# A trunk of one layer on one core: the head by steps, gate stores two products later, part loads by GpSimd, normalising in steps

## The chip, the cores and the metric

The kernel runs on one core of a Trainium2 chip. The metric is the time of one execution on the device in microseconds (us). The five engines of a core are named as the profile names them: PE (matrix products), DVE (vectors), ACT (activations and casts), POOL (GpSimd) and SP (which here only issues transfers). Each engine runs its own instructions in the order of its queue; semaphores tie the queues together.

## The reference

One layer of a decoder trunk over 2048 positions of width 1024, in float32:

```python
mod = silu(c) @ w_ada + b_ada                       # 3 x 1024
shift, scale, gate = split(mod, 3)
u = x * (1 + scale) + shift
q, k, v, a_gate, p_in, p_gate, m_a, m_p = split(u @ w_in)
a = sliding_window_sink_attention(q, k, v, sinks, bias, mask) * silu(a_gate)
a = a @ w_attn_proj
p = einsum('bsgc,gcd->bsgd', multiscale_causal_pool(p_in), w_pool_mix)
p = ((p * pool_scale) * silu(p_gate)) @ w_pool_proj
y = (sigmoid(m_a) * a + sigmoid(m_p) * p) @ w_out * (1 + gate)
x = layer_norm(2 ** 0.25 * x + y, ln_gain, ln_bias)
```

The attention has 16 query heads of width 64, two key and value heads, a window of 128, a bias by distance and one sink per head. The pool is a causal mean over 2, 4, 8 or 16 positions less the position itself.

## The kernel before

**Products.** Every large matrix product is done by seven half-size products instead of eight, in the manner of Strassen and Winograd. The activation side is held as seven "sets" (B11, T1, T2, B21, T3, B22, T4: blocks of the input and differences of blocks), the weight side is combined per use. A `Quad` is the work of two weight tiles of 128 columns: it loads their four parts (A11, A21, A22, then A12 in `mid`, line 281), POOL combines them (lines 275, 279, 280, 285), ACT and DVE split each combination into a high and a low part in a reduced format (ACT's cast at line 307, DVE's subtract at line 128), and PE multiplies 12 times 128x512 per product. `front` does the products B11 and T1 of a quad, `back` the other five of each quad of a group. A group is two quads, 14 products. After each product `tick` runs the hooks that were planned for this place.

**Phases.** Each half of the sequence (1024 positions) goes through a gates phase (g0, g1: attention gate, pool gate and the two merge gates are computed, activated and stored to memory), and an attention phase (a0, a1: queries are computed, attention is done in blocks, the pool runs beside it on DVE and POOL). Then the mix phases project attention and pool results of both halves, and the output phase multiplies with `w_out` in four groups and normalises the rows. At each boundary the seven sets of the next phase are filled or built, half by half, at planned ticks.

**Order of the work.** A scheduler orders what is issued as `nc.sync`, `nc.scalar`, `nc.vector`, `nc.gpsimd`. What is issued through `sp`, `act`, `dve`, `pool` is kept in program order. Tiles come from pools with tags: the tag "c" has five buffers in turn, "p" four, "spare" two, "wide0" to "wide7" one each; a new tile waits until the old content of its buffer has been read or stored.

**Head.** `head` computes `silu(c)`, then for k = 0 to 7 the shift and the scale of 128 channels: the shift by 16 matmuls of one column on PE into one PSUM bank (`sums`), the scale as a row sum on DVE (`tensor_tensor_reduce`), each added to the bias in `mod`. ACT modulates x with them. From k and k+4 the parts of the sets follow: `sets_a` (B11, T1), `sets_b` (B21, T2), `sets_c` (B22, T3, T4), each split by ACT and DVE, the differences made by POOL. `products(i)` runs those matmuls of the first four products whose channels are there. `bias_rows` writes the attention's bias rows by 32 small POOL operations and stores them.

**Gates, A12, rows.** `gate_quad` activates a product's result on ACT (line 456), finishes it on DVE (lines 458, 460) and stores it on SP (line 461). `mid` issues the A12 load on SP behind POOL's subtract of line 279 or 280. In the output phase `out_quad` loads a row tile z when its first half is there (line 503), adds the product (line 508), and with the second half done goes through the whole normalisation at once: sum (ACT, 512), mean and its negative (DVE), squares (ACT, 516), power (POOL, 518), scaling with gain and bias (DVE, 519 and 520), store (ACT's queue, 521).

## Time and profile before

Three executions took 1890.62, 1895.62 and 1894.25 us, the median is 1894.25 us.

| what | value |
|---|---|
| profiled execution, its own time | 1898.95 us |
| its span | 1897.2 us |
| mean granted clock of PE | 0.968 |
| busy: PE, DVE, ACT, POOL | 92%, 69%, 50%, 49% |
| instructions | 25359 |
| bytes moved by DMA | 381.33 MB |

A row of a timeline has its start, its duration, the engine, the line, the operation, the tile it writes and those it reads, the shapes and how often it runs in sequence; in brackets stands how long the engine was idle before and what ended that. A row of the waits has the engine, the tile and line that waited, what it waited for, then the total in us, how many times, and the longest. A window has the busy time of PE, PEld, DVE, ACT and POOL in that stretch, with the number of instructions, then the granted clock, the share of the DMA engines and GB/s. In the kernel many operations are recorded under one helper line (55), so that tile names tell them apart: `pv`, `pt`, `lg`, `mm` are PSUM banks, `w_set` the split weights, `W` and `A` their raw parts, `set_B` and `set_T` the sets, `sig` the gates, `wide` the rows.

### The profile page before, as it was taken

The numbers are of one execution on the slowest core, as the hardware profiler recorded it, in microseconds if no ns is written. First come the engines' busy times: TensorE is split into PE (matmuls) and PEld (weight loads), VectorE is DVE, ScalarE is ACT, GpSimd is POOL, SyncE is SP. The second block draws the span as 40 slices with busy tenths as digits, with TensorE's granted clock in tenths as the row PEclk, the third lists the DMA queues.
The fourth block names the chain that finished last, engine by engine and source line by source line (L and its number), as shares of the span: only waits on it lengthen the run. The fifth ranks groups of instructions, "written<-read, shape, count | busy, mean of one in ns | idle before, by whom it ended". The sixth has DMA issues, their size and how long they took to land. (4 is left out here: it accounts for less than half of the span.)

```text
span 1897.2 us, 25359 instructions
## 1 busy us (share of the span) xinstructions
PE 1748.8 (92%) x8248; PEld 1446.6 (76%) x8248; DVE 1301.5 (69%) x2261; ACT 942.3 (50%) x1974; POOL 923.7 (49%) x724
## 2 busy tenths in 40 slices
PE   4589999999999999899999999999989989999996
PEld 4467777777888887677777888888867768777775
DVE  4767675564677776677665457777758987857776
ACT  3444434343777776444444457777725333423443
POOL 3544444441254666435354324457743764566542
PEclk9689999999999999999999999999989999999998
DMA  6344656568254447676767733543776574588332
GB/s 244 128 172 177 233 183 233 201 247 216 87 161 151 146 158 275 243 252 220 255 242 268 248 119 128 167 167 117 285 266 240 197 244 164 197 323 319 144 134 89
DMA packets 167284, 381.33 MB, mean 201 GB/s; under 512 B 19680, under 2 KB 23792, under 8 KB 167152
## 3 DMA queue, kind: packets, MB, share of 16 engines
q1 hardware_dynamic: 156288, 348.72, 52.7%
q0 software_dynamic: 5472, 17.85, 2.6%
q10 hardware_dynamic: 5392, 13.14, 2.0%
q8 instruction: 65, 1.06, 0.2%
q14 instruction: 67, 0.55, 0.1%
HBM read 244.35 MB, written 138.44 MB: 202 GB/s over the span
## 5 line engine op out<-in xcount | busy, mean ns | idle before, releaser
L55 PE MATMUL mm<-set_B,w_set 128*128 128x512 f32 x3240 | 813.3, 399 | 29.5 <-DVE w_set L128 25.1
L55 PEld LDWEIGHTS mm<-set_B,w_set 128*128 128x128 f32 x3240 | 610.0, 191 | 163.9 <-DVE w_set L128 34.2
L55 PE MATMUL lg<-set_T,w_set 128*128 128x512 f32 x2088 | 527.7, 402 | 59.2 <-DVE w_set L128 24.6
L55 PEld LDWEIGHTS lg<-set_T,w_set 128*128 128x128 f32 x2088 | 397.4, 193 | 166.7 <-DVE w_set L128 39.0
L128 DVE TENSOR_TENSOR w_set<-W,w_set 128x1024 fp32r<-128x1024 f32 x164 | 236.1, 1439 | 99.3 <-ACT w_set L307 89.7
L307 ACT CAST w_set<-W 128x1024 fp32r<-128x1024 f32 x164 | 171.8, 1048 | 218.2 <-PE mm L55 148.3
L55 PE MATMUL mm<-set_T,w_set 128*128 128x512 f32 x1080 | 268.8, 397 | 0.0
L55 PEld LDWEIGHTS mm<-set_T,w_set 128*128 128x128 f32 x1080 | 204.0, 191 | 42.6
L285 POOL TENSOR_TENSOR W<-W 128x512 f32<-128x512 f32 x58 | 79.9, 1377 | 169.1 <-DVE w_set L128 164.5
L279 POOL TENSOR_TENSOR W<-W 128x512 f32<-128x512 f32 x56 | 88.0, 1571 | 142.7 <-DVE w_set L128 122.9
L55 DVE TENSOR_TENSOR o<-pv,o 64x128 f32<-64x128 f32 x256 | 72.2, 282 | 99.6 <-ACT o L55 95.6
L358 POOL TENSOR_TENSOR p<-p,u 128x512 f32<-128x512 f32 x58 | 87.2, 1505 | 96.1 <-DVE u L357 91.8
L55 ACT ACTIVATE L<-L,nm 128x257 f32<-128x257 f32 (+1 forms) x256 | 127.1, 498 | 8.8 <-DVE nm L55 3.5
L55 DVE TENSOR_TENSOR k_lo<-spare,k_hi 128x512 fp32r<-128x512 f32 x88 | 83.9, 957 | 65.6 <-ACT k_hi L55 31.9
L275 POOL TENSOR_TENSOR W<-W,A 128x512 f32<-128x512 f32 x56 | 80.0, 1429 | 87.6 <-DMA W<-in_win_dram 23.8
L55 DVE CUSTOM_DVE_ANT_0 L<-lg,bt,nsink 128x256 f32<-128x256 f32 (+1 forms) x256 | 111.6, 473 | 5.3 <-PE lg L55 1.3
L55 POOL TENSOR_TENSOR w_set<-W,w_set 128x1024 fp32r<-128x1024 f32 x14 | 33.7, 2408 | 146.5 <-ACT w_set L55 108.5
L280 POOL TENSOR_TENSOR W<-W 128x512 f32<-128x512 f32 x56 | 90.9, 1623 | 22.9 <-DMA W<-in_win_dram 19.7
L55 POOL TENSOR_TENSOR p<-nxt,pg 128x512 f32<-128x512 f32 x32 | 41.3, 1292 | 123.2 <-DVE sm L55 113.6
L55 ACT COPY o<-pv 64x256 f32<-64x256 f32 x128 | 47.2, 369 | 80.6 <-PE pv L55 76.4
L55 DVE TENSOR_TENSOR ptl<-pt,pth 128x512 fp32r<-128x512 f32 (+1 forms) x128 | 85.6, 669 | 1.7 <-ACT pth L55 1.6
L55 ACT CAST k_hi<-spare 128x512 fp32r<-128x512 f32 x88 | 53.9, 616 | 60.3 <-POOL spare L55 29.7
(168 smaller groups left out, 2524.6 us busy)
## 6 DMA issues: line engine op xcount, KB each, us to landing
W<-in_win_dram SPq DMA_DIRECT2D x102, 256.0 KB, 3.8
w_set<-wmix_d SPq DMA_DIRECT2D x32, 512.0 KB, 5.4
A<-in_win_dram SPq DMA_DIRECT2D x34, 256.0 KB, 4.0
ag_d<-sig SPq DMA_DIRECT2D x32, 256.0 KB, 2.7
pg_d<-sig SPq DMA_DIRECT2D x32, 256.0 KB, 3.3
ma_d<-sig SPq DMA_DIRECT2D x32, 256.0 KB, 3.0
mp_d<-sig SPq DMA_DIRECT2D x32, 256.0 KB, 3.5
pg<-pg_d SPq DMA_DIRECT2D x32, 256.0 KB, 3.9
```

Of the source, the lines that this page charges most:

```text
L55: return lambda *args, **kw: self.tc.keep_in_program_order(op(*args, **kw))
L128: engine.tensor_tensor(dst, src, as32(hi), ALU.subtract)
L275: e.tensor_tensor(x[:, 1, :], x[:, 2, :], self.a22, ALU.add)
L279: e.tensor_tensor(x[:, 1, :], x[:, 1, :], x[:, 0, :], ALU.subtract)
L280: e.tensor_tensor(x[:, 2, :], x[:, 0, :], x[:, 2, :], ALU.subtract)
L285: nc.gpsimd.tensor_tensor(x[:, 0, :], x[:, 0, :], x[:, 1, :], ALU.subtract)
L307: a.copy(by_two(hi), raw)
L358: nc.gpsimd.tensor_tensor(p5, p5, u2, ALU.add)
```

## The change

- **Head.** `sets_a`, `sets_b`, `sets_c` are replaced by one loop over i = 0 to 3, in which the steps of one pair (i, i+4) stand between those of the next: `minus`, `parts`, `rest_sums`, `rest_parts`. PE's sums go to four banks in turn (`pv`, `pt`, `lg`, `lg`), and for k = 3 and 7 DVE does them instead. The loads of x land in tiles of other tags. `bias_rows` moves to the fourth tick of the first group of gates, in program order on POOL, its load to SP.
- **Gates.** The store of a gate is deferred by two ticks (`defer`, `run_due`) and issued in program order on SP.
- **A12.** `mid` issues the load through GpSimd.
- **Normalising.** `norm_row` does one step per tick: sum, squares, power, scale, store, in program order on each engine, the store on SP. Six rows are loaded at the start of the phase (`load_z`), each next one three ticks after a store, into six tiles in place of five. The scratch of the squares is a "spare" tile.
- **Order of tiles.** At the start of the mix T3 is allocated ahead of T4, and wide4 to wide7 at once; in attention the second pool part comes one step later, but for the last.

```diff
-        def mid(self, q=nc.sync, e=nc.gpsimd):
+        def mid(self, q=nc.gpsimd, e=nc.gpsimd):
...
+    now, due = [0], []
+    def defer(ticks, f):
+        due.append((now[0] + ticks, len(due), f))
+    def run_due(every=False):
+        while due and (every or any(d[0] <= now[0] for d in due)):
+            d = min(due, key=lambda d: d[:2])
+            due.remove(d)
+            d[2]()
...
+            now[0] += 1
+            run_due()
...
-        return after(tick) if after else None
+        result = after(tick) if after else None
+        if not (after and nxt):
+            run_due(True)
+        return result
...
-            nc.sync.dma_start(gates_d[name][s, m + mi, t], g)
+            defer(2, lambda: sp.dma_start(gates_d[name][s, m + mi, t], g))
...
+    zs = {}
+    def load_z(ph, row):
+        if row < S // P:
+            zs[row] = [wide(ph, 2 + row % 6), 0]
+            sp.dma_start(zs[row][0], xr[row * P : (row + 1) * P, :])
+    def norm_row(ph, row, z):
+        def small(name):
+            return ph.t.tile([P, 1], F32, tag=name, bufs=2, name=name)
+        total, mean, down, rs = (small(x) for x in ("total", "mean", "down", "rs"))
+        def sums():
+            act.activation(z, z, AF.Copy, accum_out=total)
+        def squares():
+            dve.tensor_scalar(mean, total, 1.0 / D, None, ALU.mult)
+            dve.tensor_scalar(down, total, -1.0 / D, None, ALU.mult)
+            act.activation(ph.spare(), z, AF.Square, bias=down, accum_out=rs)
+        def power():
+            dve.tensor_scalar(rs, rs, 1.0 / D, EPS, ALU.mult, ALU.add)
+            pool.tensor_tensor(rs, rs, mhalf, ALU.pow)
+            dve.scalar_tensor_tensor(z, z, mean, vec["gain"], ALU.subtract, ALU.mult)
+        def scale():
+            dve.scalar_tensor_tensor(z, z, rs, vec["lnb"], ALU.mult, ALU.add)
+        def store():
+            sp.dma_start(out[row * P : (row + 1) * P, :], z)
+            defer(3, lambda: load_z(ph, row + 6))
+        for at, f in ((1, sums), (2, squares), (3, power), (4, scale), (5, store)):
+            defer(at, f)
     def out_quad(k):
-        zs = {}
-        def small(ph, name):
-            return ph.t.tile([P, 1], F32, tag=name, bufs=2, name=name)
         def consume(ph, mi, n, src):
-            r0 = (k + mi) * P
-            if mi not in zs:
-                z = wide(ph, 2 + (k + mi) % 5)
-                nc.sync.dma_start(z, xr[r0 : r0 + P, :])
-                zs[mi] = [z, 0]
-            z = zs[mi][0]
-            zs[mi][1] += 1
+            z, n_done = zs[k + mi]
+            zs[k + mi][1] += 1
             zn = z[:, n * CH : (n + 1) * CH]
             nc.vector.scalar_tensor_tensor(zn, zn, ALPHA, src, ALU.mult, ALU.add)
-            if zs[mi][1] < 2:
-                return
-            total, mean, down, rs = (small(ph, x) for x in ("total", "mean", "down", "rs"))
-            nc.scalar.activation(z, z, AF.Copy, accum_out=total)
-            nc.vector.tensor_scalar(mean, total, 1.0 / D, None, ALU.mult)
-            nc.vector.tensor_scalar(down, total, -1.0 / D, None, ALU.mult)
-            sq = wide(ph, 7)
-            nc.scalar.activation(sq, z, AF.Square, bias=down, accum_out=rs)
-            nc.vector.tensor_scalar(rs, rs, 1.0 / D, EPS, ALU.mult, ALU.add)
-            nc.gpsimd.tensor_tensor(rs, rs, mhalf, ALU.pow)
-            nc.vector.scalar_tensor_tensor(z, z, mean, vec["gain"], ALU.subtract, ALU.mult)
-            nc.vector.scalar_tensor_tensor(z, z, rs, vec["lnb"], ALU.mult, ALU.add)
-            nc.scalar.dma_start(out[r0 : r0 + P, :], z)
+            if n_done:
+                norm_row(ph, k + mi, z)
...
-        act.dma_start(rel, relT)
+        nc.sync.dma_start(rel, relT)
         et = ph.t.tile([HEADS, ET], F32, tag="c", bufs=ph.bufs["c"], name="et")
-        nc.gpsimd.memset(et, BIG)
+        pool.memset(et, BIG)
...
-            nc.gpsimd.tensor_scalar(
+            pool.tensor_scalar(
                 et[:, lo_t : hi_t + 1], rel[:, b : b + 1].to_broadcast([HEADS, n]), -1.0, None, ALU.mult
             )
-        nc.gpsimd.dma_start(e_d, et)
+        pool.dma_start(e_d, et)
...
-                if n % U == 4 + 2 * st and (j, st) in sums:
+                if n % U == ((4, 6 + (j + 1 < KT))[st]) and (j, st) in sums:
...
-        cg = ph.p("cg"), ph.p("cg")
+        cg = [t for t in (places[5][:, 0:CH], places[5][:, CH:])]
...
-        bias_rows(ph)
-        sums = bank("pv")
         ws, xs, ts = {}, {}, {}
+        by_pe = (0, 4, 1, 5, 2, 6)
...
-            sp.dma_start(ws[k][0], wadat[k])
+            sp.dma_start(ws[k][0], (wadat if k in by_pe else wada)[k])
...
-            if k < 4:
-                xs[k] = (ph.spare(),)
-                sp.dma_start(xs[k][0], xt[0, k])
-            else:
-                xs[k] = ph.p("b21"), ph.p("b22")
-                for h, x in enumerate(xs[k]):
-                    sp.dma_start(x, cols(xt[0, k], h))
+            if k in (0, 1, 6):
+                t = ph.spare()
+                xs[k] = cols(t, 0), cols(t, 1)
+                sp.dma_start(t, xt[0, k])
+                return
+            xs[k] = [ph.p("x") if k in (4, 5, 7) else ph.c("x") for h in range(2)]
+            for h, x in enumerate(xs[k]):
+                sp.dma_start(x, cols(xt[0, k], h))
+        sums = {}
+        def pe_modulation(k):
+            if k not in by_pe:
+                return
+            sums[k] = bank(("pv", "pt", "lg", "lg")[by_pe.index(k) % 4])
+            for i in range(KT):
+                mm(sums[k][:, 0:1], ws[k][0][:, i * P : (i + 1) * P], ct[:, i : i + 1], start=i == 0, stop=i == KT - 1)
         def modulation(k):
-            wt, wa = ws.pop(k)
-            for i in range(KT):
-                mm(
-                    sums[:, k : k + 1],
-                    wt[:, i * P : (i + 1) * P],
-                    ct[:, i : i + 1],
-                    start=i == 0,
-                    stop=i == KT - 1,
-                    skip_group_check=True,
-                )
+            for m, wa in ((KT + k, ws[k][1]), (k, ws[k][0])):
+                if m in by_pe:
+                    dve.tensor_tensor(mod[:, k : k + 1], mod[:, k : k + 1], sums[k][:, 0:1], ALU.add)
+                else:
+                    dve.tensor_tensor_reduce(
+                        wa, wa, cb, 1.0, mod[:, m : m + 1], ALU.mult, ALU.add, mod[:, m : m + 1]
+                    )
             m = KT + k
-            dve.tensor_tensor_reduce(
-                wa, wa, cb, 1.0, mod[:, m : m + 1], ALU.mult, ALU.add, mod[:, m : m + 1]
-            )
-            dve.tensor_tensor(mod[:, k : k + 1], mod[:, k : k + 1], sums[:, k : k + 1], ALU.add)
...
-        eng = act, dve
-        def sets_a(i):
-            xa = xs[i][0]
-            split_set("B11", i, cols(xa, 0), eng=eng)
-            t = ts[i] = ph.last(True)
-            pool.tensor_tensor(t, cols(xa, 1), cols(xa, 0), ALU.subtract)
-            split_set("T1", i, t, eng=eng)
-        def sets_b(i):
-            b21, b22 = xs[4 + i]
-            split_set("B21", i, b21, eng=eng)
-            pool.tensor_tensor(ts[i], b22, ts[i], ALU.subtract)
-            split_set("T2", i, ts[i], eng=eng)
-        def sets_c(i):
-            (xa,), (b21, b22), t = xs[i], xs[4 + i], ts[i]
-            pool.dma_start(b12_d[i // 2, :, i % 2, :], cols(xa, 1))
-            pool.tensor_tensor(cols(xa, 0), t, cols(xa, 0), ALU.subtract)
-            pool.tensor_tensor(b21, b21, t, ALU.subtract)
-            split_set("B22", i, b22, eng=eng)
-            split_set("T3", i, cols(xa, 0), eng=eng)
-            split_set("T4", i, b21, eng=eng)
+        def minus(dst, a, b):
+            pool.tensor_tensor(dst, a, b, ALU.subtract)
+        def parts(name, i, src):
+            split_set(name, i, src, eng=(act, dve))
+        def rest_sums(i):
+            b11, b12 = xs[i]
+            b21, t = xs[4 + i][0], ts[i]
+            pool.dma_start(b12_d[i // 2, :, i % 2, :], b12)
+            minus(b11, t, b11)
+            minus(b21, b21, t)
+        def rest_parts(i):
+            parts("B22", i, xs[4 + i][1])
+            parts("T3", i, xs[i][0])
+            parts("T4", i, xs[4 + i][0])
...
+        load_x(1)
+        pe_modulation(0)
+        pe_modulation(4)
         modulation(0)
-        load_x(1)
-        sets_a(0)
-        for q in grp:
-            starts.append(pair_split(ph, q.first(), act, dve))
-        modulation(4)
         load_w(5)
         load_x(5)
-        sets_b(0)
-        modulation(1)
-        load_w(2)
-        products(0)
-        sets_a(1)
-        sets_c(0)
-        load_x(2)
-        modulation(5)
-        load_w(6)
-        load_x(6)
-        sets_b(1)
-        modulation(2)
-        load_w(3)
-        products(1)
-        sets_a(2)
-        sets_c(1)
-        load_x(3)
-        modulation(6)
-        load_w(7)
-        load_x(7)
-        sets_b(2)
-        for q in grp:
-            q.mid(sp, pool)
-        modulation(3)
-        modulation(7)
-        products(2)
-        sets_a(3)
-        sets_b(3)
-        products(3)
-        return groups, turn, opened, cb, lambda: (sets_c(2), sets_c(3))
+        for i in range(4):
+            t = ts[i] = ph.last(True)
+            minus(t, xs[i][1], xs[i][0])
+            parts("B11", i, xs[i][0])
+            if i > 0:
+                rest_sums(i - 1)
+            modulation(4 + i)
+            if i == 0:
+                load_w(2)
+                load_x(2)
+            if i == 1:
+                load_w(3)
+                load_x(3)
+            parts("T1", i, t)
+            minus(t, xs[4 + i][1], t)
+            if i < 3:
+                pe_modulation(i + 1)
+                pe_modulation(i + 5)
+            parts("B21", i, xs[4 + i][0])
+            if i == 0:
+                for q in grp:
+                    starts.append(pair_split(ph, q.first(), act, dve))
+            if i in (1, 2):
+                grp[i - 1].mid(pool, pool)
+            products(i)
+            if i < 3:
+                modulation(i + 1)
+            if i < 2:
+                load_w(6 + i)
+            parts("T2", i, t)
+            if i > 0:
+                rest_parts(i - 1)
+            if i == 1:
+                load_x(6)
+                load_x(7)
+        rest_sums(3)
+        return groups, turn, opened, cb, lambda: rest_parts(3)
...
-        at(0, 0, rest)
+        at(0, 1, rest)
+        at(0, 3, lambda: bias_rows(ph))
...
-    def late_sets(pl):
-        sets["T4"], sets["T3"] = set_tile(pl, "T4"), set_tile(pl, "T3")
+    def late_sets(pl, *names):
+        for n in names:
+            sets[n] = set_tile(pl, n)
     with Pools("g0", spare=2, p=4, c=5) as ph:
-        late_sets(ph.t)
+        late_sets(ph.t, "T4", "T3")
...
-        late_sets(ph.t)
+        late_sets(ph.t, "T4", "T3")
...
-        late_sets(ph.t)
+        late_sets(ph.t, "T3", "T4")
+        for k in range(4, KT):
+            ta[k] = wide(ph, k)
...
-            if i % 2 == 0:
+                for row in range(6):
+                    load_z(ph, row)
+            if i in (2, 4):
...
```

## The prediction

> **What bounds the kernel now.** I read the page's busy shares first, then the windows, then what TensorE (PE) waited for, then the timelines of PE and of the engines it names.
>
> ```profile
> span 1897.2 us, 25359 instructions
> PE 1748.8 (92%) x8248; PEld 1446.6 (76%) x8248; DVE 1301.5 (69%) x2261; ACT 942.3 (50%) x1974; POOL 923.7 (49%) x724
> PE   4589999999999999899999999999989989999996
> ```
>
> The span is PE's: 92% busy, and the slices show where it is not, at the head, in dents, and at the end. At most 1897.2 − 1748.8 = 148.4 us of idle time can be won, beside matmuls that ran at a low clock. In the windows the columns are busy PE, PEld, DVE, ACT, POOL, then PE's granted clock:
>
> ```profile
> 0.00:100.00 100.00, 55.18 (x227) 47.83 (x228) 56.62 (x101) 40.12 (x60) 46.22 (x70) 0.80 0.48 177
> 500.00:600.00 100.00, 99.49 (x567) 86.42 (x566) 74.97 (x236) 74.31 (x226) 46.39 (x38) 1.00 0.45 145
> 1800.00:1900.00 100.00, 76.57 (x318) 61.13 (x316) 67.27 (x98) 38.15 (x60) 36.82 (x26) 0.90 0.30 112
> ```
>
> Attention (500 to 600) has half a microsecond to give: the attention edit can win nothing there. The first 100 us leave PE idle for 45, the last for 23 (2.8 of them beyond the span's end, and much of the rest the tail of the last row). What PE waited for:
>
> ```profile
> PE pv L55 <- DVE mod L55: 25.6, 4, 12.3
> PE mm L55 <- DVE w_set L128: 25.1, 13, 4.2
> PE lg L55 <- DVE w_set L128: 24.6, 30, 2.4
> PE lg L55 <- ACT w_set L307: 24.3, 16, 9.8
> ```
>
> 25.6 us in four waits are the modulation matmuls of the head, each waiting until VectorE (DVE) has read the bank's last sums. The other three rows, 74 us, are weight splits that come late.
>
> **Head (45 us idle).** These are the first and last of the four waits, and the stalls behind the head:
>
> ```profile
> 28.10 3.58 PE L55 MATMUL pv<-ct,head_vv 128*128 128x1 f32 x16 [12.25 <-DVE mod L55]
> 65.24 3.57 PE L55 MATMUL pv<-ct,head_kk 128*128 128x1 f32 x16 [3.82 <-DVE mod L55]
> 77.70 2.60 PE L55 MATMUL lg<-set_T,w_set 128*128 128x512 f32 x10 [0.35 <-DVE w_set L128]
> 92.80 1.22 PE L55 MATMUL lg<-set_T,w_set 128*128 128x512 f32 x2 [9.78 <-ACT w_set L307]
> 94.36 4.18 PE L55 MATMUL lg<-set_T,w_set 128*128 128x512 f32 x10 [0.34 <-DVE w_set L128]
> ```
>
> With four banks the bank wait goes. What is late next is DVE, ACT and GpSimd (POOL), which make the input parts step by step:
>
> ```profile
> 9.72 1.28 DVE L55 CUSTOM_DVE_ANT_0 head_kk<-head_kk,cb,mod 128x1024 f32<-128x1024 f32 x1
> 11.46 6.57 POOL L560 TENSOR_SCALAR et<-rel 16x1 f32<-16x1 f32 x32 [9.80 <-DMA rel<-in_relT_dram]
> 81.91 4.12 DVE L55 TENSOR_TENSOR set_T<-spare,set_T 128x512 fp32r<-128x512 f32 x1 [0.82 <-ACT set_T L55]
> ```
>
> Two k now sum on DVE: 2 × 1.28 = 2.6 us more there, for 2 × 3.6 less on PE. The 6.57 us of bias rows leave POOL's queue here, but its weight adds wait for loads anyway, so I count 2 of them. A step on DVE: two row sums of 1.28, seven subtracts of half that width at about 0.65 by the same row, and its share of the two extra sums, 7.7 us. Four are 31. But in each, DVE waits in turn for ACT's casts, POOL's subtract and the loads, by my chaining some 3 us: 10.8. The first difference that a T1 part needs came from POOL behind the bias rows (11.46 + 6.57 = 18.0) and the weight adds; without the bias rows it comes at about 21. 21 + 4 × 10.8 = 64 for the end of the fourth step's products, 65 with what PE then still has to do; before, they end near 76.7 (two matmuls and 0.35 ahead of 77.70): −12. At 92.80 ACT was behind five casts of the late sets; each step now casts its predecessor's, which should cut the 9.78 to some 3, but the products in front of it also come sooner, so I count nothing on top. Bounds: −22 (also the 9.78 goes, and the slow ten at 94.36) and −5: the 81.91 row shows a subtract of half a row that took 4.12 us while POOL ran its own back to back, and the steps now mix more of both. I take −12, nearer the middle, since four bank waits alone are 25.6 and about half of that should fall to the next cover.
>
> The bias rows return in the first group of gates with two buffers of the ring that the mix weights' low and high parts reuse: these then wait for 6.57 us of POOL work and a store. From 0 to +8; I take +2, as these parts are off PE's path until several products later.
>
> **Gate stores two products later, A12 loads by POOL.** SP's queue is where these stand:
>
> ```profile
> SPq L281 <- POOL W L279: 170.5, 49, 14.9
> SPq L461 <- ACT sig L456: 129.6, 43, 10.2
> 309.74 0.81 DVE L55 TENSOR_SCALAR spare<-spare,mod 128x1024 f32<-128x1024 f32 x1 [5.37 <-DMA spare<-in_xt_dram]
> 312.34 4.14 PE L55 MATMUL mm<-set_B,w_set 128*128 128x512 f32 x10 [2.31 <-DVE w_set L128]
> ```
>
> SP stands at L281 and L461 for 300 us with the other loads behind it. Mostly that costs nothing, but at 309.74 an x load landed 5.37 late, DVE stood, and PE lost 2.31 plus some 1.5 of slow matmuls (ten took 4.14; at 77.70 ten took 2.60). In the changed order the x loads stand ahead of stores and weight loads. This place and two smaller ones of the kind: −6 for both halves (0 to −12).
>
> A store two products late (5.4 us) keeps its ring buffer that much longer: 128 stores. Where a sigmoid already waited for a buffer, it is small, and I take 0 (0 to +6, the ring's waits doubled once less than half):
>
> ```profile
> ACT sig L456 <- DMA ma_d<-sig: 11.3, 5, 3.8
> ```
>
> At both ends of attention the A12 load stood behind the set fills on SP's queue:
>
> ```profile
> 748.54 1.04 ACT L55 CAST w_set<-W 128x1024 fp32r<-128x1024 f32 x1 [4.13 <-DMA W<-in_win_dram]
> 750.74 0.55 PE L55 MATMUL pv<-pth,vv 128*128 128x256 f32 x1 [3.64 <-DVE o L55]
> 1377.64 1.04 ACT L55 CAST w_set<-W 128x1024 fp32r<-128x1024 f32 x1 [3.34 <-DMA W<-in_wap_dram]
> 1379.85 0.36 PE L55 MATMUL pv<-pth,vv 128*128 128x256 f32 x1 [2.85 <-DVE o L55]
> ```
>
> ACT stood 4.13 and 3.34 us with attention's own casts behind it, and PE lost 3.64 and 2.85. On a queue of its own the load isn't behind the fills: −6.5, of which I take −6 (0 if it shares the transfer engines with them all the same, to −10 with the slow matmuls behind).
>
> The cost of the move is POOL's. Its DMA issues of the same kind (an attention-free stage; the durations are ns):
>
> ```profile
> L487 POOL DMA_DIRECT2D y_d<-wide x32: 767/767/785, 1476.4 to 1723.0; - x32
> DMA to landing us min/median/max: 2.7/4.4/7.2
> W<-in_win_dram SPq DMA_DIRECT2D x102, 256.0 KB, 3.8
> 1797.63 0.32 SPq L281 DMA_DIRECT2D W<-y_d  x1
> 1806.77 1.04 ACT L307 CAST w_set<-W 128x1024 fp32r<-128x1024 f32 x1 [1.31 <-DVE rs L517]
> ```
>
> 58 loads × 0.77 = 45 us of POOL time. POOL is half idle, and what follows in its queue (weight adds, p sums) feeds work some products later; if the cover goes, it is 0.77 each. I charge a tenth: +4 (0 to +15). Landing 4.4 instead of 3.8 is well inside the 9.1 us that lie between issue at 1797.63 and the cast at 1806.77.
>
> [...]
>
> **Mix and the way into the output.** Three rows:
>
> ```profile
> 1389.61 8.27 PE L55 MATMUL mm<-set_B,w_set 128*128 128x512 f32 x24 [4.00 <-ACT u L348]
> 1706.83 0.69 DVE L483 TENSOR_TENSOR gp<-c,gp 128x512 f32<-128x512 f32 x1 [8.25 <-DMA gp<-mp_d]
> 1710.60 4.63 PE L55 MATMUL mm<-set_B,w_set 128*128 128x512 f32 x10 [4.21 <-DVE w_set L128]
> ```
>
> At 1389.61 ACT's copy waited for stores whose buffers it inherits. With T3, T4 and the wide tiles allocated in another order it inherits older ones; the T3 fill then waits next. I take −3 (0 to −6). At 1706.83 DVE waited 8.25 for a load that stood behind the loads of LayerNorm rows, which themselves wait for the last y stores; PE lost 4.21 and some 2 of slow matmuls. These rows are now loaded behind the gate loads: −5 (0, if the six rows hold up the next fills, to −6.5).
>
> **Normalising in steps.**
>
> ```profile
> 1776.12 2.88 PE L55 MATMUL mm<-set_B,w_set 128*128 128x512 f32 x12
> 1778.84 2.88 PE L55 MATMUL lg<-set_T,w_set 128*128 128x512 f32 x12
> 1810.53 3.94 PE L55 MATMUL lg<-set_T,w_set 128*128 128x512 f32 x10 [1.92 <-DVE w_set L128]
> 1854.37 3.48 PE L55 MATMUL lg<-set_T,w_set 128*128 128x512 f32 x10 [1.93 <-DVE w_set L128]
> ```
>
> One product is 2.72 us (1778.84 − 1776.12). A group has 14, 38.1 us, and takes 43.84 (1854.37 − 1810.53): 5.8 over. The split that PE waits for stands on ACT behind squares that wait for DVE (1806.77, above: 1.31 <-DVE rs), and on DVE behind the row's last scale. In steps of one product each, at most one sum and one square stand ahead of it, and it should be ready before its product. Three boundaries of 3.5 to 4.5, less what stays of the folding: −10 (−4 to −14). The tail stays: the last row's steps run without products between.
>
> [...]
>
> **Sum.** Head −12, bias +2, x loads and queue −6, ends of attention −6, POOL issues +4, mix −3, way into the output −5, normalising −10: −36. The profiled execution took 1898.95 us, 4.7 above the median of 1894.25, so 1858 from the median. 0.3%, 5.7 us, is about what a measurement of this kernel tells from no change.
>
> **Rivals.**
> A, the gains fall on the next cover (chance 0.25): the head wins 5 (DVE and POOL stretch each other, as at 81.91), x loads and attention ends 3 together, mix 0, boundary −2, normalising −6, with the +6 of POOL and bias: −10, so 1884. For it: each stall has DVE or ACT as its releaser, and both keep their work. Against: the last boundary's causes are orders, not work.
>
> B, slower (0.1): A12 loads arrive too late from POOL. Issued behind POOL's own waits and landing in up to 7.2 us, they hold the second split of each pair, and everything in DVE's and ACT's order behind it. With 36 − 10 = 26 us left of gains elsewhere, it decides from (26 + 6)/58 = 0.55 us per load; at 0.77 + 0.6 (issue on the path, and the later median) each of 58 costs 1.37, 79 us, less 30 of gains: 1943; at half of it 1904. Against: the 9.1 us of slack.
>
> C, everything pays (0.1): head −20, normalising −13, ends −10, queue −10, mix and boundary −10, issues +2: −61, so 1833.
>
> D, it does nothing that PE feels (0.05): SP's waits are idle time of an engine that isn't the bound, and the head is bound by its DVE work: 1894.
>
> **The numbers.** My case has 0.5. Its own range is 1844 to 1877, the distances from each taken value to its ends added as independent ones (14 below, 19 above). Faster by over 0.3%: 0.5 + 0.1 + 0.22 of A = 0.82, within 0.3%: 0.03 of A and 0.03 of D, so 0.06, slower: 0.1 of B and 0.02 of D, 0.12. The range for all is 1836 to 1892: it leaves out B and D and the far side of C.
>
> **What would show it.** Right: no wait of PE for DVE's mod in the head and the products of the first step before 30 us; the wait at the ends of attention for W gone; SP's waits at the stores and at L281 gone; the group period of the output near 40. Wrong: POOL's wait for its own issues ahead of L280 or L358, PE waits "ACT w_set <- DMA W" in number, sigmoids waiting for stores for much more than 11.3 us, T3's fill holding PE longer at the start of mix, or DVE subtracts in the head above 1 us each.

## The result, and the profile after

The changed kernel takes 1880.25 us in the median of four runs (1876.43 to 1884.18), the kernel before 1894.74 (1890.62 to 1895.62). The ratio is 0.9928, its interval 0.9901 to 0.9955: some 14 us faster, where 36 were forecast. The time lies within the stated range (1836 to 1892); the gain is far from the forecast one. In a later set on another chip the ratio was 0.9878 (0.9845 to 0.9911). Chips differ by more than half a per cent (the kernel before took from 1894.74 to 1906.64 us in the medians of these sets), so each kernel below is given as a ratio to the kernel before on its own chip, and traces are set side by side where they come from one chip.

The page of the changed kernel, its first lines:

```profile
span 1876.5 us, 25257 instructions
PE 1736.9 (93%) x8216; PEld 1438.0 (77%) x8216; DVE 1320.7 (70%) x2263; ACT 939.9 (50%) x1978; POOL 954.5 (51%) x782
PE   6489899999999999899999999999989979989997
```

PE's idle time fell only from 148.4 to 139.6 us (1876.5 − 1736.9). What it waited for has changed, though; the longest of these waits:

```profile
PE lg L55 <- DVE w_set L128: 22.0, 25, 2.4
PE mm L55 <- DVE w_set L128: 20.3, 14, 2.8
PE lg L55 <- ACT w_set L307: 20.1, 16, 4.0
PE mm L55 <- DVE set_B L55: 9.5, 2, 5.2
PE mm L55 <- ACT set_B L55: 8.9, 2, 5.6
PE mm L55 <- ACT set_T L55: 6.5, 2, 3.3
```

The bank wait of the head (25.6 us on DVE's mod) is gone, and in its place stand 24.9 us in which PE waits for the parts themselves, set_B and set_T. The split waits only shrank, from 74.0 to 62.4.

Where the time came from is seen best from a row that occurs once per quad: DVE's sum of a product at line 382 (line 357 for the first row). These are starts in us, from a trace of each kernel on the same chip (spans 1898.3 and 1877.9):

| DVE's row | before | changed | difference | step |
|---|---|---|---|---|
| first T2 product summed (357) | 80.5 | 88.4 | +7.9 | +7.9 |
| end of the first group of gates, 2nd row of 382 | 133.1 | 136.2 | +3.1 | −4.8 |
| end of g0, 16th row | 464.5 | 468.8 | +4.3 | +1.2 |
| first group of g1, 18th row | 788.1 | 783.3 | −4.8 | −9.1 |
| end of g1, 34th row | 1097.3 | 1086.9 | −10.4 | −5.6 |
| first group of mix, 36th row | 1416.5 | 1402.1 | −14.4 | −4.0 |
| last group but one of mix, 48th row | 1669.7 | 1655.8 | −13.9 | +0.5 |
| first group of the output, 52nd row | 1754.3 | 1744.7 | −9.6 | +4.3 |
| last row | 1884.2 | 1863.9 | −20.3 | −10.7 |

The head and the way into the output lost; attention, g1 and the output groups won. Two traces of one kernel differ by up to 3 us in such a step (from the 16th to the 18th row the kernel before took 320.7 us in its first trace, 323.7 in this one), so the steps of +1.2 and +0.5 tell nothing.

### The profile page after: what moved, and what is told of

Read it like the earlier page. It is cut to its first block, busy times and chain, and to the rows that moved or that the text cites. A ratio compares the mean times of both kernels' runs of the same rounds, so it can differ in the third digit from the quotient of the medians.

```text
span 1876.5 us, 25257 instructions
## 1 busy us (share of the span) xinstructions
PE 1736.9 (93%) x8216; PEld 1438.0 (77%) x8216; DVE 1320.7 (70%) x2263; ACT 939.9 (50%) x1978; POOL 954.5 (51%) x782
## 5 line engine op out<-in xcount | busy, mean ns | idle before, releaser
L55 PE MATMUL mm<-set_B,w_set 128*128 128x512 f32 x3240 | 808.9, 398 | 38.7 <-DVE w_set L128 20.3
L285 POOL TENSOR_TENSOR W<-W 128x512 f32<-128x512 f32 x58 | 79.4, 1368 | 161.7 <-DVE w_set L128 147.9
L358 POOL TENSOR_TENSOR p<-p,u 128x512 f32<-128x512 f32 x58 | 93.6, 1615 | 87.9 <-DVE u L357 83.2
L55 DVE TENSOR_TENSOR k_lo<-spare,k_hi 128x512 fp32r<-128x512 f32 x88 | 88.2, 1008 | 53.9 <-ACT k_hi L55 28.8
L280 POOL TENSOR_TENSOR W<-W 128x512 f32<-128x512 f32 x56 | 92.4, 1650 | 20.6 <-DMA W<-in_win_dram 17.7
```

What stands on the lines that cost most here:

```text
L55: return lambda *args, **kw: self.tc.keep_in_program_order(op(*args, **kw))
L280: e.tensor_tensor(x[:, 2, :], x[:, 0, :], x[:, 2, :], ALU.subtract)
L285: nc.gpsimd.tensor_tensor(x[:, 0, :], x[:, 0, :], x[:, 1, :], ALU.subtract)
L358: nc.gpsimd.tensor_tensor(p5, p5, u2, ALU.add)
```

## Experiments: parts undone

**The head of before in the changed kernel.** `head` and `bias_rows` are those of before, the late parts stand at the first tick.

```diff
-        at(0, 1, rest)
-        at(0, 3, lambda: bias_rows(ph))
+        at(0, 0, rest)
```

> The changed kernel with the head of before (batches, one bank, bias rows in the head). By the traces the changed head is 8.2 us late at the first T2 product and 2.4 us late at the end of the first group, so without it the kernel should be 2 to 3 us faster than the changed one: some 17 us under before. By the prediction's term (head -12) it should be some 10 us slower than the changed one, 2 to 4 us under before.

Measured: ratio 0.9884 (0.9863 to 0.9905). Between the two ratios of the changed kernel, so this run alone doesn't decide; it speaks against a new head that is worth 10 us, for without it the ratio should then be 0.993 or more.

**A12 loads on SP again.**

```diff
-        def mid(self, q=nc.gpsimd, e=nc.gpsimd):
+        def mid(self, q=nc.sync, e=nc.gpsimd):
```

> The changed kernel with the A12 loads of the rings on SP again (those of the head stay on GpSimd). If the queue of its own is what freed the ends of attention, ACT waits for W again there (4.1 and 3.3 us before) and the kernel loses 4 to 8 us there; if GpSimd's issues delay the last y stores and with them the stop of 11.5 us on ACT at the last mix group, it wins up to 7 us there. Sum between -3 and +6 against the changed kernel; the prediction's terms (ends -6, issues +4) give +2.

Measured: 0.9878 (0.9862 to 0.9894): no slower than the changed kernel, where the prediction's terms gave +2. By the traces attention, from its first scores to its last value product on PE, takes 270.9 and 272.9 us here in its two halves; in the next two kernels, on the same chip and with the loads on GpSimd, it takes 267.7 to 268.0 and 271.2 to 271.3. So the queue of its own does win some 5 us at the ends of attention, and loses at least as much elsewhere.

**Gates stored at once.**

```diff
-            defer(2, lambda: sp.dma_start(gates_d[name][s, m + mi, t], g))
+            nc.sync.dma_start(gates_d[name][s, m + mi, t], g)
```

> The changed kernel with each gate stored at once, in the scheduler's order. By the prediction (x loads and queue -6, half of it the stores) 3 us slower than the changed kernel, SP's wait at the stores back near 230 us. By the traces the first gates phase won nothing (+0.4 us) and the second 2.1, so 0 to 2 us slower. If the longer hold of the buffers costs, it is faster.

Measured: 0.9943 (0.9923 to 0.9963), slower than the changed kernel by 3 to 12 us, as its two ratios are taken (3 is within the intervals, 12 isn't). SP waits 298 us for gates to be finished, where it waited 156 in the changed kernel and 230 in the kernel before. In this order of the loads the deferred store pays; the forecast of 3 is at the low end. In the first gates phase this kernel needs 10.7 us more than the next one on the same chip, which has the same gates part with deferred stores (the rows of line 357 of the second and the last group there: 150.0 to 460.5 against 150.0 to 449.8).

**Rows normalised at once.** `out_quad` and the row loads are those of before.

> The changed kernel with the rows normalised at once and loaded as before. By the traces the output phase won 8.6 us, so 8 to 10 us slower than the changed kernel, with the group period near 43.8 us again. If the row loads ahead of time are what holds up the last mix group, part of its 3.8 us comes back and it is 5 us slower.

Measured: 0.9948 (0.9932 to 0.9963), 4 to 13 us slower than the changed kernel. From the 52nd row of line 382 to the last its trace takes 131.5 us, the changed kernel's 119.2 and the kernel before 129.9.

**The changed kernel once more, and the kernel before on the same chip.**

> The changed kernel as it is, beside the same runs of the kernel before as the other kernels of this set. It should repeat a ratio of 0.990 to 0.9955; only with it can the kernels with one part undone be set against it on one chip.

> The kernel before, for a trace on the same chip as the others of this set: ratio 1 within 0.3%.

Measured: 0.9878 (0.9845 to 0.9911), and one run of 1900.1 us beside a median of 1900.34. The traces of the table above are these two.

**Old head and A12 on SP together.**

> The changed kernel with both the head of before and the A12 loads of the rings on SP. If the two parts cost independently, it wins over the changed kernel what both win alone, by the first set's ratios 0.4 and 0.5%, so a ratio near 0.984 (1864 us where before takes 1895). If A12 on its own queue is what frees the ends of attention, it is no better than the old head alone: 0.988.

Measured: 0.9840 (0.9809 to 0.9870), 1869.87 us beside 1877.96 for the changed kernel on the same chip. Two parts of the change that were forecast to win 10 (the head with its bias rows) and 2 us win 8 when they are undone. The old head is 8.8 us ahead at the first T2 product and 2.8 at the end of the first group; between the rows of line 357 of the 47th and the 51st quad, where the output begins, another 7.5 us are won, of which 4.3 are left by the table's rows (48th to 52nd: 84.6 us, 88.9 in the changed kernel).

**Second pool part of attention at step 6 again.**

```diff
-                if n % U == ((4, 6 + (j + 1 < KT))[st]) and (j, st) in sums:
+                if n % U == 4 + 2 * st and (j, st) in sums:
```

> The changed kernel with the second pool part of attention at step 6 again. By the traces attention's period of 16 blocks went from 33.2 to 32.7 us, 2.5 us in each half, so this is 5 us slower than the changed kernel if that edit did it. By the prediction (attention has nothing to give) there is no difference; then another part made attention faster.

Measured: 0.9931 (0.9904 to 0.9958), 1887.85 us, 10 us over the changed kernel beside it. The windows from 500 to 600 us of the kernel before, the changed one and this one, on one chip:

```profile
500.00:600.00 100.00, 99.50 (x569) 86.55 (x568) 74.71 (x234) 74.09 (x225) 46.39 (x38) 1.00 0.45 145
```

```profile
500.00:600.00 100.00, 100.00 (x579) 87.88 (x578) 75.48 (x237) 75.06 (x228) 46.95 (x39) 1.00 0.45 142
```

```profile
500.00:600.00 100.00, 99.49 (x570) 86.53 (x569) 75.32 (x236) 74.46 (x226) 46.40 (x38) 1.00 0.45 145
```

The idle share is only half a per cent, and yet 569 matmuls became 579 in the same 100 us. Part of that is where the window cuts; the period says it exactly. In the first half PE starts the scores of every 16th block 33.2 us apart before, 32.8 in the changed kernel and 33.2 with the step undone; in the second half it is 33.7, 33.3 and 33.7. One place in each period makes most of it. These are rows of DVE and PE there from the same traces, first of the kernel before, then of the changed one; `nxt` is the second pool part, `pth` and `ptl` are the high and low parts that PE multiplies next:

```profile
505.90 0.69 DVE L55 SCALAR_TENSOR_TENSOR nxt<-nxt,mm 128x512 f32<-128x512 f32 x1
507.99 0.68 DVE L55 TENSOR_TENSOR ptl<-pt,pth 128x512 fp32r<-128x512 f32 x1
508.26 0.28 PE L55 MATMUL pv<-pth,vv 128*128 128x256 f32 x1
508.73 0.39 PE L55 MATMUL pv<-ptl,vv 128*128 128x256 f32 x1 [0.19 <-DVE ptl L55]
```

```profile
511.82 0.68 DVE L55 TENSOR_TENSOR ptl<-pt,pth 128x512 fp32r<-128x512 f32 x1
512.68 0.68 DVE L55 SCALAR_TENSOR_TENSOR nxt<-nxt,mm 128x512 f32<-128x512 f32 x1
512.57 0.28 PE L55 MATMUL pv<-pth,vv 128*128 128x256 f32 x1
512.69 0.29 PE L55 MATMUL pv<-ptl,vv 128*128 128x256 f32 x1
```

Before, the pool part stands ahead of `ptl` in DVE's queue, and PE starts its second product 0.47 us after the first instead of 0.12; the profile shows only 0.19 of that as idle. With the pool part behind `ptl` the wait is gone, and with the step undone it is back once in each period. From the first scores of attention to the last, the changed kernel takes 256.1 and 260.6 us in the two halves, this one 260.7 and 264.4: 8.4 us, of which 3.3 lie in the last periods, where the medians differ by 10.

## Experiments: the head

These are the head's products in the changed kernel, PE's timeline:

```profile
45.24 0.50 PE L55 MATMUL mm<-set_B,w_set 128*128 128x512 f32 x1 [3.25 <-ACT set_B L55]
50.92 1.22 PE L55 MATMUL mm<-set_B,w_set 128*128 128x512 f32 x2 [5.18 <-DVE set_B L55]
65.32 0.80 PE L55 MATMUL mm<-set_B,w_set 128*128 128x512 f32 x1 [5.64 <-ACT set_B L55]
70.42 1.22 PE L55 MATMUL mm<-set_B,w_set 128*128 128x512 f32 x2 [4.30 <-DVE set_B L55]
77.91 1.48 PE L55 MATMUL mm<-set_T,w_set 128*128 128x512 f32 x3
```

The second step was done at 42 us, as forecast (21 + 2 × 10.8 = 42.6); the third and fourth took 17.7 and 19.7 us where I had 10.8, and the last ended at 79.4 instead of 64. Two things stand in front of them, a stretched subtract on DVE and on ACT a wait for x of k = 6, whose load waits for the buffer of the first pair:

```profile
43.81 5.25 DVE L55 TENSOR_TENSOR set_B<-x,set_B 128x512 fp32r<-128x512 f32 x1
63.22 4.74 DVE L55 TENSOR_TENSOR set_T<-A,set_T 128x512 fp32r<-128x512 f32 x1 [2.09 <-ACT set_T L55]
53.33 1.52 ACT L55 ACTIVATE spare<-spare,mod 128x512 f32<-128x512 f32 x2 [8.14 <-DMA spare<-in_xt_dram]
```

POOL's subtracts during the first of these rows, which ends half a microsecond after them:

```profile
44.22 1.27 POOL L55 TENSOR_TENSOR A<-x 128x512 f32<-128x512 f32 x1
46.01 1.27 POOL L55 TENSOR_TENSOR spare<-A,spare 128x512 f32<-128x512 f32 x1
47.23 1.27 POOL L55 TENSOR_TENSOR x<-x,A 128x512 f32<-128x512 f32 x1
```

**x of k = 6 sooner.** The first pair's late parts are made a step earlier, so that its buffer comes free. This kernel also loads the weights of k = 7 over those of k = 2 before these are summed, so one modulation has another value; the amount of work is the same.

```diff
             parts("B21", i, xs[4 + i][0])
+            if i == 1:
+                rest_parts(0)
+                load_w(7)
+                load_x(6)
...
-            if i < 2:
-                load_w(6 + i)
+            if i < 1:
+                load_w(6)
...
-            if i > 0:
+            if i > 1:
                 rest_parts(i - 1)
             if i == 1:
-                load_x(6)
                 load_x(7)
```

> The changed head, with the first pair's B22, T3 and T4 parts made one step earlier, so that the load of x for k=6 is issued some 8 us sooner (ACT waited 8.1 us for it). If this wait makes the third step late, the first T2 product comes 5 to 8 us earlier (83 instead of 88 us). If the subtracts stretched beside GpSimd make it late, 0 to 2 us.

The same two rows of ACT's and DVE's timelines in this kernel:

```profile
52.67 1.52 ACT L55 ACTIVATE spare<-spare,mod 128x512 f32<-128x512 f32 x2 [5.20 <-DVE mod L55]
62.56 4.74 DVE L55 TENSOR_TENSOR set_T<-A,set_T 128x512 fp32r<-128x512 f32 x1 [2.09 <-ACT set_T L55]
```

The load's wait is gone, DVE's mod took its place, and ACT starts 0.7 us sooner. The first T2 product is summed at 87.5 us, 88.4 in the changed kernel; the ratio is 0.9915 (0.9899 to 0.9931). The load alone isn't the cause; the stretched subtract is still there.

**Differences on DVE.**

```diff
         def minus(dst, a, b):
-            pool.tensor_tensor(dst, a, b, ALU.subtract)
+            dve.tensor_tensor(dst, a, b, ALU.subtract)
```

> The changed head with all its differences made by DVE instead of GpSimd: 16 more operations of about 0.7 us on DVE (11 us), but no subtract beside GpSimd's own; those stretched ones are 18 us over their length in the trace. If the stretching makes the steps late, the first T2 product comes 5 to 10 us earlier; if the load of x for k=6 does, 0 to 3 us earlier; if DVE's work itself, later.

Measured: 0.9842 (0.9829 to 0.9855). DVE and PE at the third step:

```profile
42.82 0.69 DVE L55 TENSOR_TENSOR set_B<-x,set_B 128x512 fp32r<-128x512 f32 x1
44.63 0.69 DVE L55 TENSOR_TENSOR A<-x 128x512 f32<-128x512 f32 x1
45.83 0.69 DVE L55 TENSOR_TENSOR spare<-A,spare 128x512 f32<-128x512 f32 x1
```

```profile
45.97 1.22 PE L55 MATMUL mm<-set_B,w_set 128*128 128x512 f32 x2 [1.08 <-DVE set_B L55]
69.52 1.48 PE L55 MATMUL mm<-set_T,w_set 128*128 128x512 f32 x3
70.80 3.46 PE L55 MATMUL lg<-set_T,w_set 128*128 128x512 f32 x12
```

The subtract that took 5.25 us takes 0.69, and a difference costs DVE 0.69, where the 16 of them cost POOL 1.3 to 1.7 each. The fourth step's products end at 71 us, the first T2 product is summed at 75.3, 13 us sooner than in the changed kernel, and the first group ends at 122.3, 10.8 ahead of the kernel before. The third and fourth steps take 13.5 and 16.0 us here; the forecast 10.8 and DVE's four differences of 0.69 make 13.6. The run also takes POOL's slower difference and its handover out of each step, so not all of the 13 us is the stretching: the two stretched rows are 8.6 us over 0.69 each, and the two steps got 7.9 shorter. The head's term of −12 comes out near its size here, but in part by luck: at the end of the fourth step's products 5.9 us are won (71.0 against 76.9), and the other 5 come in the rest of the first group, for which I had counted nothing.

**The changed head alone, in the kernel before.**

> The kernel before with the changed head alone (bias rows in the first group of gates), nothing else changed. By the traces the first T2 product comes 8 us later and the first group ends 2 to 3 us later: 2 to 5 us slower than before. By the prediction: 10 us faster.

Measured: 1.0027 (1.0011 to 1.0042), 5 us slower. The first T2 product is summed at 88.6 us, the first group ends at 136.2.

## Experiments: A12 and the way into the output

**A12 by GpSimd alone, in the kernel before.** The edit is that of `mid`, backwards.

> The kernel before with the A12 loads of the rings issued by GpSimd, nothing else changed. By the prediction the waits of ACT for W at both ends of attention go and it is 2 us faster (ends -6, issues +4). If the issues delay the y stores and the weight sums in GpSimd's queue, it is up to 8 us slower.

Measured: 1.0029 (1.0012 to 1.0045), 5.5 us slower. The trace kept of it is of the fastest of twelve executions (1899.03 us, the median is 1908.33), so it shows the waits, not where the 5.5 us are lost. These rows of line 281 are first of the kernel before, then of this one: the issue, who waited for it, and the time to landing.

```profile
L281 SPq DMA_DIRECT2D W<-in_win_dram x32: 328/333/934, 132.6 to 1063.0; - x32
  ACT w_set L307: 7.1, 4
  ACT w_set L55: 5.9, 2
DMA to landing us min/median/max: 2.5/3.1/9.4
```

```profile
L281 POOL DMA_DIRECT2D W<-in_win_dram x32: 557/557/578, 131.6 to 1057.8; - x32
  POOL W L279: 14.2, 48
  ACT w_set L307: 36.7, 13
  ACT w_set L55: 1.3, 1
DMA to landing us min/median/max: 2.8/3.7/6.7
```

At the ends of attention the wait fell from 5.9 to 1.3 us, as forecast; but elsewhere ACT now waits 36.7 us in 13 casts instead of 7.1 in 4. Each load holds POOL for 0.56 us and 0.30 more before it (14.2 over 48, POOL waiting for its own subtract to be done).

**The way into the output.** In the changed kernel:

```profile
1663.04 0.58 ACT L348 COPY u<-mm 128x512 f32<-128x512 f32 x1 [11.48 <-DMA y_d<-wide]
1664.62 5.91 PE L55 MATMUL lg<-set_T,w_set 128*128 128x512 f32 x12 [4.01 <-ACT w_set L307]
1692.07 0.69 DVE L499 TENSOR_TENSOR gp<-c,gp 128x512 f32<-128x512 f32 x1 [3.97 <-DMA gp<-mp_d]
1697.65 2.92 PE L55 MATMUL mm<-set_B,w_set 128*128 128x512 f32 x6 [2.14 <-DVE w_set L128]
```

The wait that I had named is halved (8.25 to 3.97, and PE's 4.21 to 2.14). But 30 us ahead of it ACT stands 11.48 us: the load of `ln_bias` (issued on ACT's queue at 1662.66) waits for the y stores of its buffer. In the kernel before it stood 7.29 us at this place, and PE lost nothing. POOL, which makes and issues the y stores, has A12 loads between them now; with the old head and A12 on SP the stop is 7.78 us.

**Gain and bias loads in program order on SP.**

```diff
-                    nc.scalar.dma_start(vec[name], src.partition_broadcast(P))
+                    sp.dma_start(vec[name], src.partition_broadcast(P))
```

> The changed kernel with the two loads of gain and bias of the rows issued in program order on SP instead of on ACT's queue. In the traces ACT stood 11.5 us behind the second of them, until the last y stores of the group before had landed, and PE lost 4.0 us and some 3 of slow matmuls at the start of the last mix group. If that is the cause of the loss on the way into the output, the wait goes and the stage is 4 to 7 us shorter; if another load takes its place, 0 to 2.

Measured: 0.9896 (0.9877 to 0.9915), between the two ratios of the changed kernel; 4 us are 0.2%, which these intervals can't tell. ACT's stop is gone, and the 51st quad comes 5.6 us sooner than by the distance up to there (7.1 us behind the changed kernel's trace at the 47th quad, 1.5 at the 51st, on different chips). By the table's rows, 48th to 52nd, 3.7 of them are left (85.2 us, 88.9 in the changed kernel). Then PE waits twice for the B22 set, 2.1 us together, which it did not before; the first of the two:

```profile
1729.44 1.66 PE L55 MATMUL mm<-set_B,w_set 128*128 128x512 f32 x6 [1.15 <-DMA set_B<-wo_B_split]
```

**Old head, A12 on SP and these loads on SP.**

> The old head, A12 loads on SP, gain and bias loads in program order on SP, the rest as changed. Against the old head with A12 on SP (0.984) up to 7 us less where ACT stood 7.8 us there: a ratio of 0.980 to 0.984.

Measured: 0.9843 (0.9829 to 0.9856): no better than without the last edit (0.9840).

**Differences on DVE and A12 on SP, then with the four loads at attention's ends by GpSimd.**

```diff
-                nxt_group[n // 62].mid()
+                nxt_group[n // 62].mid(nc.gpsimd)
```

> The changed kernel with the head's differences on DVE and the A12 loads of the rings on SP. The first gave 0.984 where the changed kernel gives about 0.990, the second won 5 to 8 us on the way into the output: if both hold together, a ratio of 0.978 to 0.982; if A12 by GpSimd is needed at the ends of attention, 0.984 or more.

> The kernel with the head's differences on DVE and A12 on SP, once more on the same chip as the one beside it: a ratio of 0.978 to 0.983.

> The kernel with the head's differences on DVE and A12 on SP, but the four A12 loads at the ends of the two attention phases by GpSimd. There ACT waited 8.5 us for W in two casts with SP, and 1.3 with GpSimd. If the queue of its own pays only there, 3 to 6 us less than with all on SP; if the waits behind (the T3 fill) take it over, 0 to 2.

Measured: 0.9805 (0.9783 to 0.9828) and 0.9791 (0.9771 to 0.9811) for the first, 0.9771 (0.9748 to 0.9795) for the second, 1865.92 and 1863.8 us on one chip. Both are some 40 us under the kernel before and beat the changed one. Whether the ends of attention bring anything of their own stays unclear: 2 us, within the intervals. By the traces attention is 3.3 and 1.3 us shorter with the four loads by GpSimd, and the second gates phase, whose code is the same, 5.9 longer (18th to 34th row: 305.0 and 299.1); the one trace is of the slowest of its executions and the other of the fastest.

## Why the prediction was wrong

- **Head, −12: the step that failed.** "In each, DVE waits ... by my chaining some 3 us: 10.8." The cost that it leaves out is that DVE's subtract takes several times its 0.69 us while POOL runs subtracts beside it: the row that I had shown for the bound, 4.12 us beside POOL's, came back in this head with 5.25 and 4.74 us in the two steps (subtracts above 1 us were named as a sign of being wrong). The third and fourth steps took 17.7 and 19.7 us. With the differences on DVE the first group ends 10.8 us ahead of before; with them on POOL, 3.1 behind. The term should have been +3 to +5; together with the bias rows (+2 there, not run apart) the head alone measured +5. My bounds, −22 and −5, left out a loss although the row for it was quoted.
- **POOL issues, +4, and ends of attention, −6: the first mis-sized.** Each mechanism was there: the wait at the ends fell from 5.9 to 1.3 us, and POOL paid 0.86 us a load (0.77 forecast). In the traces attention is some 5 us longer with A12 on SP again (3 in its first half, 2 in its second), so most of the −6 is there. Some of it passes on to the set fills: behind the first half PE waits 4.9 us for T's parts with A12 by GpSimd alone, and 3.1 at this place before. What failed is "well inside the 9.1 us that lie between": one slack at one place of the output stood for all, and 13 casts elsewhere waited, 36.7 us. The two terms together were −2; alone they measured +5.5. If some 3 of these 5 stay won, the issues cost some 8 to 9, not 4; this is an estimate from these numbers. It is rival B's mechanism far under its price: PE's own listed waits grew only from 137.9 to 143.1 us in the traces.
- **DVE's subtracts beside POOL's.** In the third step DVE's subtract from two tiles took 5.25 us (43.81 to 49.06) while POOL ran three of its own (44.22 to 48.50), and 0.69 with the differences on DVE. POOL's three took 1.27 us each, its other differences in this head 1.26 to 1.66, so the added length is DVE's alone. What makes it so long, no view here shows. POOL's 32 issues of A12 loads in the gates and attention took 554 to 579 ns in the changed kernel.
- **Gate stores and x loads, −6: right in sign.** g0 and g1 together won 4.4 us in the two traces of one chip, with A12's cost in them, all of it in g1; storing at once costs 3 to 12. In eight traces of kernels with the changed code of g1 it took 303.7 to 309.1 us by these rows, on several chips, and in the two of the kernel before 309.1 and 309.2, so the size is open. SP's waits at the stores, which were to go, fell from 230 to 156 us; the sigmoids did not pay for it (their waits for `ma_d` stores went from 11.3 to 2.5 us).
- **Attention, 0: wrong, and in the kernel's favour.** "Attention has half a microsecond to give" took the busy share for the speed. A wait of 0.19 us in each period, with 0.35 us between two starts behind it, was worth 8.4 us in both halves by the traces, 10 by the medians. Without this gain, which was not forecast, the change wins 12 us instead of 22 on that chip (1887.85 and 1877.96, the kernel before 1900.34).
- **Mix, −3: nothing won.** The copy at its start (4.00 us of PE's) waits no longer, but PE now waits there for T3, as the step said would be late next. It does so with A12 on SP too (3.77), so it belongs to this part; I had priced what is left too low. No run undoes the order of tiles alone.

```profile
1380.04 4.18 PE L55 MATMUL lg<-set_T,w_set 128*128 128x512 f32 x10 [4.48 <-DMA set_T<-ain_T_split]
```

- **Way into the output, −5: +4.3.** The named wait was halved (8.25 to 3.97 us), but the load of `ln_bias` on ACT's queue, which waits for the y stores, became critical: ACT stood 11.48 us there, 7.29 before, and PE lost 4.01. With A12 on SP again ACT stands 7.78 us with the old head, and 9.34 with the changed head's differences on DVE; with the old head and A12 on SP this stage is 4.3 us shorter again.
- **Normalising, −10: right.** 10.7 us between the first group of the output and the last row (8.6 in the first two traces); the group's period by rows of line 357 is 41.9 and 39.6 us (1760.5, 1802.4, 1842.0) where it was 44.7 and 44.5 (1770.6, 1815.2, 1859.7). The tail stayed: 14.0 us from the last sum to the end, 14.1 before.

Of the rivals, A gave the time best (1884 for 1880): the gains did fall on the next cover, in the head by DVE's subtracts, 5.25 and 4.74 us beside POOL's, as it said of DVE. Not as it said, POOL's own kept their length (1.26 to 1.28 us beside these two), the head lost, normalising paid in full, the way into the output lost and attention won; that the time came within 4 us of its own is luck in part.

## What to carry to other kernels

Before work is put side by side, look at which engines share it: a subtract of DVE from two tiles beside POOL's own took more than seven times its length (5.25 us against 0.69), so a slow row in the trace of before belongs in the middle of the estimate when the change makes more such pairs. One measured slack holds at its place; a load moved for all of its 56 uses in the rings needs the tightest of them. And where an engine is busy for 99.5%, look for a short wait that comes back in every period, and count the instructions in a window, before saying that nothing can be won.

## What was unexpected in the hardware

A transfer issued by POOL behind its own subtract cost 0.56 us (557 to 578 ns in 32 issues) and 0.30 of waiting, and landed 0.6 us later in the median than from SP (3.7 against 3.1). DVE's subtract of 128x512 took 0.69 us, and 2.9 to 5.3 us at seven places in the heads before and after the change where POOL ran two or three subtracts beside it; POOL's own subtracts stayed at 1.3 to 1.7 in the changed head.
